# Values first, the output gate later, and longer attention waits in a two-block transformer on one core

## The chip, the core and the metric

The kernel runs on one core of a Trainium2 chip. A core has engines that work side by side, each with its own queue of instructions, taken in order: PE (TensorE) multiplies matrices and transposes, DVE (VectorE), ACT (ScalarE) and POOL (GpSimd) work on vectors, SP issues DMAs. An instruction that needs another engine's result waits for a semaphore, and everything behind it in its own queue waits with it. The metric is the device time of one launch in microseconds (us), the median of several runs.

## The reference

Two blocks of two layers each work on `x` of 256 rows and 1024 columns, all in float32. Cut to what matters here:

```
def first_block(x, ...):
    for l in range(2):
        z = rms_norm(x, attn_norm_g[l]) @ w_in[l]
        qa, ka, va, qb, kb, vb, ga, gb = split(z, [512, 128, 128, 512, 512, 512, 1024, 1024])
        qa, ka = rope(rms_norm(qa, q_norm_a)), rope(rms_norm(ka, k_norm_a))     # norm per head of 64
        ya = window_gqa(qa, ka, va, sink_a[l]) @ w_proj_a[l]                    # 8 heads, 2 of keys
        qb, kb = rms_norm(qb, q_norm_b), rms_norm(kb, k_norm_b)
        yb = neighbourhood_attn(qb, kb, vb, rel_bias_b[l]) @ w_proj_b[l]        # 8 heads
        x = x + (sigmoid(ga) * ya + sigmoid(gb) * yb) @ w_out[l]
        x = x + swiglu(rms_norm(x, ffn_norm_g[l]))

def second_block(x, ...):
    for l in range(2):
        q_a, k_a, v_a, x_m, z_m = split(x @ w_in[l], 512 each)
        y_a = dilated_attention(q_a, k_a, v_a, rel_bias)                        # 8 heads, causal
        x_c = silu(causal_conv(x_m))
        h = layer_norm(mlstm(x_c, x_m), per head) * m_norm_g
        y_m = sigmoid(z_m) * h
        g_a, g_m = split(sigmoid(x @ w_gate[l] + b_gate[l]))
        y = (g_a * (y_a @ w_br_a[l]) + g_m * (y_m @ w_br_m[l])) @ w_o[l]
        x = layer_norm(ALPHA * x + y)
        x = layer_norm(ALPHA * x + (swiglu(x) if l == 0 else moe(x)))           # moe: 8 experts, 2 of them each row
```

## The kernel before

**Matmuls.** The rows are two halves of 128, `t` = 0 and 1. Every weight comes from HBM as `raw`; ACT casts its upper part to `wh` (L218) and DVE subtracts that from it to give `wl` (L219), for 1024 columns at a time. Each product is made of three matmuls (L366 to L368: `wh` by `xTh`, `wl` by `xTh`, `wh` by `xTl`). `project` multiplies the rows by a stretch of up to 512 columns, weights block by block, and hands each finished half (in PSUM, `mm`) to a function `done(t, ps)`. With `outer=4` the last four blocks are done for half 0 first and then for half 1.

**Side work.** What is not a weight's matmul is a Python generator. `go` puts it on the list `side`, and `tick`, called after every part of `project` (two weight blocks for one half: six matmuls of 512 columns), advances each generator on it to its next `yield`. So the instructions of the side work are written among the matmuls in tick order, and engines take them in that order. `_WAIT` holds how many ticks a generator lets pass at a named place. `finish(gen)` ticks on until a generator has ended, with no matmul of weights between.

**First block.** The order of columns is q and k of the first attention (each half normalised by `head_norm`: ACT squares, DVE sums (L598), POOL takes the root (L443, L444), and after four ticks DVE multiplies (L602), which is the last reader of the PSUM buffer), then the values of the second attention (`keep_v`, columns 1792 on; the first attention's own values come with k, L844), then its q and k, then the gates. In layer 0 POOL also makes the tables of rope (L537 to L549, L540, L541), DVE the gains out of them (L586, L587) and the rotation (L609, L615, L616).

**Attention** goes in quads of four heads of one half (`softmax_quad`): scores on PE (L625), row maxima with the bias on DVE (L640), exponentials on ACT (L652), reciprocal and scaling on DVE (L656, L658), wait "s2", transposes on PE (L665), copies to SBUF by `evac`, which takes ACT (L431) and DVE (L433) in turn, wait "s3", product with the values on PE (L673), and its upper and lower parts on ACT and DVE (L677, L678). A second quad may start five ticks after the one before.

**Second block.** The order of columns is the output gate `z_m` (tanh), the convolution's input, at which the mLSTM generator `M` starts, q, k, values, at which the attention `A` starts, then four stretches of `w_gate_2`, each ended by DVE's addition of the bias (L1211) and ACT's tanh. mLSTM's output is written on DVE (L1092 to L1117). `branches` then multiplies mLSTM's output and the attention's by their weights, in this order; before the first matmul of each it calls `finish` on the generator.

Of the kernel before, what the change touches and what calls it, by code (L numbers as in the profile page):

```python
# [14 lines left out]
ALU = mybir.AluOpType  # L15
# [19 lines left out]
_WAIT = {"m15": 4, "m16": 2, "x0": 4, "t": 13, "r": 31, "g": 3, "g0": 7, "h": 3, "y": 3, "p": 2, "a0": 4, "a1": 0, "a2": 2, "q": 9, "k": 6, "b": 11, "s0": 0, "s1": 2, "s2": 4, "s3": 3, "o": 2, "mix": 3, "u": 5, "x": 3, "n0": 4, "n1": 1, "m0": 4, "m1": 1, "m2": 1, "m3": 0, "m4": 0, "m5": 2, "m6": 3, "m7": 3, "m8": 1, "m9": 4, "m10": 0, "m11": 3, "m12": 0, "m13": 7, "m14": 5}  # L35
# [233 lines left out]
class Kernel:  # L269
    def __init__(self, tc, io, upto="all", orders=None):  # L270
# [9 lines left out]
        self.ticks, self.begun, self.quads = 0, -100, 0  # L280

# [309 lines left out]
    def head_norm(self, ps, nh, scale):  # L591
# [8 lines left out]
        for _ in range(4):  # L600
            yield
# [26 lines left out]
    def softmax_quad(self, t, h0, q, k, v, bias, nk, sink, hi, lo):  # L628
# [30 lines left out]
        yield from self.wait("s2")  # L659
        PT = []  # L660
        for a in range(2):
# [4 lines left out]
            self.evac(p, pt)  # L666
            PT.append(p)
        yield from self.wait("s3")
# [11 lines left out]
    def attention(self, name, deps, q, k, v, bias, nk, sink, y, beside=None, turn=None):  # L680
# [9 lines left out]
        while jobs or live:  # L690
# [10 lines left out]
            if jobs and self.quads < (_BESIDE if beside in self.side else _QUADS) and self.ticks - self.begun > _APART:  # L701
# [5 lines left out]
                gen = self.softmax_quad(t, h0, q, k, v, bias, nk(t), sink, *out[t])  # L707
# [61 lines left out]
    def branches(self, G, which, l):  # L769

        V = self.nc.vector
        for br, (wait, y, arr, side) in enumerate(which):
# [4 lines left out]
            for n in range(2):  # L777

                def gated(t, ps):
                    z = D * side + 512 * n  # L780
# [25 lines left out]
    def first_block(self, l, xT, nxt, heads):  # L806
# [53 lines left out]
        self.project(xT, 8, W(0, 512), later(prep_q), outer=4)  # L860
        if not self.dry:
            self.stream.lead = _AHEAD
        self.project(xT, 8, W(512, 256), later(prep_k), w=256)
# [32 lines left out]
        self.project(xT, 8, W(1792, 512), keep_v)  # L896
# [249 lines left out]
    def second_block(self, l, xT):  # L1146
# [19 lines left out]
        xx, thz, convs = {}, {}, []  # L1166
# [9 lines left out]
        self.project(xT, 8, [("w_in_2", (l,), 2048, 512)], tanh_z, outer=4)  # L1176
# [3 lines left out]
        qT, kT, va = {}, {}, {}  # L1180
# [8 lines left out]
        def keep_v(t, ps):  # L1189
            va[t] = self.s2(512)  # L1190
            self.evac(va[t], ps)

        self.project_T(xT, "w_in_2", l, 0, keep(qT, 0.125))
        self.project_T(xT, "w_in_2", l, 512, keep(kT, 1.0))
        self.project(xT, 8, [("w_in_2", (l,), 1024, 512)], keep_v)
# [8 lines left out]
        ))  # L1204
        for n in range(2):
            bg = self.row(D)
            self.bcast_row(bg, io["b_gate"][l, n])
            for j in range(2):
                def gate(t, ps):
                    g = G[t][:, D * n + 512 * j : D * n + 512 * j + 512]  # L1210
                    V.tensor_tensor(g, ps, bg[:, 512 * j : 512 * j + 512], op=ALU.add)  # L1211
                    nc.scalar.activation(g, g, AF.Tanh, scale=0.5)
                self.project(xT, 8, [("w_gate_2", (l,), D * n + 512 * j, 512)], gate)
# [451 lines left out]
```

## Time and profile before

| | |
|---|---|
| median of 3 runs | 2345.89 us (2345.5 to 2346.64) |
| profiled execution | 2344.98 us, span 2343.2 us |
| mean granted clock of PE | 0.990 |
| PE busy | 2269.1 us (97%) |
| DVE busy | 1822.2 us (78%) |
| ACT busy | 1441.0 us (61%) |
| POOL busy | 100.3 us (4%) |

The span is the time from the first instruction to the last one on the core. A share is that of the span in which the engine had an instruction in work. The first block's layers, the second block's layer 0 and the token mixer of its layer 1 fill the span to about 1340 us; the experts follow.

### The profile page before, as it was taken

What the parts mean: (1) busy time and instruction counts of PE and PEld (TensorE: products, weight loads), DVE (VectorE), ACT (ScalarE), POOL (GpSimd) and SP (SyncE); (2) the same over time, 40 slices, a digit from 0 to 9 for tenths busy, and PEclk for the clock granted to TensorE, in tenths of its full rate; (3) what the DMA queues carried; (4) which work ended last, traced back from release to release, by engine and by line L of the source; (5) the groups of instructions that cost most, each with busy time, mean ns of one, the idle gap of its engine ahead of it and who ended that gap; (6) DMA issues with size and microseconds to landing.
All of it is one profiled execution on the core that took longest, in us unless ns stands there. A gap on an engine that the chain in (4) does not pass through costs nothing. (4 is left out here: it accounts for less than half of the span.)

```text
span 2343.2 us, 30976 instructions
## 1 busy us (share of the span) xinstructions
PE 2269.1 (97%) x11041; PEld 1859.9 (79%) x11041; DVE 1822.2 (78%) x2672; ACT 1441.0 (61%) x2166; POOL 100.3 (4%) x163
## 2 busy tenths in 40 slices
PE   6999999999999999999998899999999999999997
PEld 5778888778888977788886688888888888888775
DVE  5866556867565677655767799999999999999988
ACT  4555444555444554444454488888888888888775
POOL 4100001100010000000100000000000000000000
PEclk9999999999999999999999899999999999999998
DMA  6435555435565444554544799999999999999981
GB/s 238 159 138 180 182 186 204 167 126 180 180 233 205 154 136 168 197 198 164 184 168 141 300 362 371 354 370 349 371 349 370 349 373 341 376 339 376 332 334 47
DMA packets 128162, 583.06 MB, mean 249 GB/s; under 512 B 14592, under 2 KB 14880, under 8 KB 74624
## 3 DMA queue, kind: packets, MB, share of 16 engines
q1 hardware_dynamic: 124416, 566.44, 66.5%
q0 software_dynamic: 3584, 14.56, 1.9%
q8 instruction: 89, 1.46, 0.2%
q14 instruction: 73, 0.60, 0.1%
HBM read 579.90 MB, written 1.05 MB: 248 GB/s over the span
## 5 line engine op out<-in xcount | busy, mean ns | idle before, releaser
L219 DVE TENSOR_TENSOR wl<-raw,wh 128x1024 fp32r<-128x1024 f32 x594 | 711.7, 1229 | 147.8 <-ACT wh L218 145.1
L366 PE MATMUL mm<-wh,xTh 128*128 128x512 f32 (+1 forms) x1904 | 762.0, 400 | 6.7 <-DVE s L602 3.3
L367 PE MATMUL mm<-wl,xTh 128*128 128x512 f32 (+1 forms) x1904 | 742.5, 390 | 8.8 <-DVE wl L219 8.8
L218 ACT CAST wh<-raw 128x1024 fp32r<-128x1024 f32 x594 | 611.9, 1050 | 122.6 <-PE mm L368 110.0
L366 PEld LDWEIGHTS mm<-wh,xTh 128*128 128x128 f32 x1904 | 359.3, 189 | 82.6 <-issue 11.7
L367 PEld LDWEIGHTS mm<-wl,xTh 128*128 128x128 f32 x1904 | 359.8, 189 | 76.0 <-DVE wl L219 9.9
L368 PE MATMUL mm<-wh,xTl 128*128 128x512 f32 (+1 forms) x1008 | 392.4, 389 | 2.1 <-DVE xTl L455 1.9
L366 PE MATMUL mm<-wh,s 128*128 128x512 f32 x968 | 386.2, 399 | 0.0
L368 PE MATMUL mm<-wh,s 128*128 128x512 f32 x968 | 378.5, 391 | 0.2 <-DVE s L458 0.2
L367 PE MATMUL mm<-wl,s 128*128 128x512 f32 x968 | 378.0, 391 | 0.0
L368 PE MATMUL mm<-wh,xTh 128*128 128x512 f32 x896 | 349.7, 390 | 0.0
L219 DVE TENSOR_TENSOR wl<-s,wh 128x512 fp32r<-128x512 f32 x384 | 242.2, 690 | 14.1 <-ACT wh L218 10.8
L219 DVE TENSOR_TENSOR wl<-wide,wh 128x1024 fp32r<-128x1024 f32 x196 | 235.1, 1222 | 17.0 <-ACT wh L218 6.2
L218 ACT CAST wh<-s 128x512 fp32r<-128x512 f32 x384 | 217.4, 620 | 23.2 <-PE mm L368 21.7
L218 ACT CAST wh<-wide 128x1024 fp32r<-128x1024 f32 x196 | 204.1, 1055 | 36.4 <-PE mm L368 33.0
L368 PEld LDWEIGHTS mm<-wh,xTl 128*128 128x128 f32 x1008 | 190.9, 189 | 43.7 <-DVE xTl L455 4.3
L366 PEld LDWEIGHTS mm<-wh,s 128*128 128x128 f32 x968 | 182.5, 189 | 39.4 <-issue 2.5
L368 PEld LDWEIGHTS mm<-wh,s 128*128 128x128 f32 x968 | 182.1, 188 | 39.7 <-DVE s L458 0.8
L367 PEld LDWEIGHTS mm<-wl,s 128*128 128x128 f32 x968 | 182.6, 189 | 35.3
L368 PEld LDWEIGHTS mm<-wh,xTh 128*128 128x128 f32 x896 | 168.3, 188 | 36.0
L454 ACT CAST s<-ax 128x256 fp32r<-128x256 f32 x178 | 66.4, 373 | 163.5 <-PE ax L452 163.5
L455 DVE TENSOR_TENSOR s<-ax,s 128x256 fp32r<-128x256 f32 x178 | 75.1, 422 | 68.2 <-ACT s L454 68.2
(287 smaller groups left out, 1934.0 us busy)
## 6 DMA issues: line engine op xcount, KB each, us to landing
raw<-in_wpre SPq DMA_DIRECT2D x197, 1024.0 KB, 4.8
wide<-in_wexp SPq DMA_DIRECT2D x97, 1024.0 KB, 6.5
s<-in_wexp SPq DMA_DIRECT2D x384, 256.0 KB, 6.4
raw<-in_wexp SPq DMA_DIRECT2D x96, 1024.0 KB, 6.6
xTl<-in_wexp SPq DMA_DIRECT2D x24, 1024.0 KB, 6.9
bc<-in_wexp SPq DMA_DIRECT2D x44, 512.0 KB, 6.9
raw<-in_wpre SPq DMA_DIRECT2D x8, 512.0 KB, 3.5
wide<-in_bias_b POOLq DMA_DIRECT2D x2, 1536.0 KB, 9.6
```

The source lines that it names most:

```text
L218: nc.scalar.copy(h, raw)
L219: nc.vector.tensor_tensor(l, raw, h.bitcast(F32), op=ALU.subtract)
L366: nc.tensor.matmul(out, xh, wh, start=first, stop=False)
L367: nc.tensor.matmul(out, xh, wl, start=False, stop=False)
L368: nc.tensor.matmul(out, xl, wh, start=False, stop=last)
L454: nc.scalar.copy(hi, ps)
L455: nc.vector.tensor_tensor(lo, ps, hi.bitcast(F32), op=ALU.subtract)
```

## The change

- `head_norm` lets five ticks pass, not four, before DVE's multiplication.
- Waits "s2" and "s3" are 5 and 4 ticks for an attention that runs beside no other generator (the first block's two), and stay 4 and 3 (`s2x`, `s3x`) in the second block's, which runs beside mLSTM.
- Both copies of transposed probabilities are on ACT.
- First block, layer 0: the second attention's values are projected first of all, with `outer=4`; layer 1 keeps its order.
- Second block: values are projected first, the output gate after k. Attention starts ahead of the gate. The gates' tanh comes a tick after the addition. `branches` takes the attention first.

```diff
--- before.py
+++ after.py
@@ -32,7 +32,7 @@
-_WAIT = {"m15": 4, "m16": 2, "x0": 4, "t": 13, "r": 31, "g": 3, "g0": 7, "h": 3, "y": 3, "p": 2, "a0": 4, "a1": 0, "a2": 2, "q": 9, "k": 6, "b": 11, "s0": 0, "s1": 2, "s2": 4, "s3": 3, "o": 2, "mix": 3, "u": 5, "x": 3, "n0": 4, "n1": 1, "m0": 4, "m1": 1, "m2": 1, "m3": 0, "m4": 0, "m5": 2, "m6": 3, "m7": 3, "m8": 1, "m9": 4, "m10": 0, "m11": 3, "m12": 0, "m13": 7, "m14": 5}
+_WAIT = {"m15": 4, "m16": 2, "x0": 4, "t": 13, "r": 31, "g": 3, "g0": 7, "h": 3, "y": 3, "p": 2, "a0": 4, "a1": 0, "a2": 2, "q": 9, "k": 6, "b": 11, "s0": 0, "s1": 2, "s2": 5, "s3": 4, "s2x": 4, "s3x": 3, "o": 2, "mix": 3, "u": 5, "x": 3, "n0": 4, "n1": 1, "m0": 4, "m1": 1, "m2": 1, "m3": 0, "m4": 0, "m5": 2, "m6": 3, "m7": 3, "m8": 1, "m9": 4, "m10": 0, "m11": 3, "m12": 0, "m13": 7, "m14": 5}
@@ -278,6 +278,7 @@
         self.ticks, self.begun, self.quads = 0, -100, 0
+        self.late = []
@@ -597,7 +598,7 @@
         nc.scalar.activation(q, v, AF.Square, scale=scale)
         nc.vector.reduce_sum(ss, q, axis=AX.X)
         r = self.rstd(ss, (nh,), 1.0 / 64, 1e-6)
-        for _ in range(4):
+        for _ in range(5):
             yield
         nc.vector.scalar_tensor_tensor(q, v, scale, r[:, :, None].to_broadcast([128, nh, 64]), op0=ALU.mult, op1=ALU.mult)
         return q
@@ -625,7 +626,7 @@
                 self.nc.tensor.matmul(ps[a][:, i], q(t, h), k(h, nk), start=True, stop=True)
         return ps
-    def softmax_quad(self, t, h0, q, k, v, bias, nk, sink, hi, lo):
+    def softmax_quad(self, t, h0, q, k, v, bias, nk, sink, hi, lo, beside):
         nc = self.nc
         V = nc.vector
@@ -656,16 +657,16 @@
         V.reciprocal(den, den)
         for a in range(2):
             V.tensor_tensor(P[a], P[a], den[:, a, :, None].to_broadcast([128, 2, nk]), op=ALU.mult)
-        yield from self.wait("s2")
+        yield from self.wait("s2" if beside is None else "s2x")
         PT = []
         for a in range(2):
             pt = self.ax(2 * nt, 128)
             p = P[a].rearrange("p a (b c) -> p (a b) c", c=128)
             for i in range(2 * nt):
                 nc.tensor.transpose(pt[:, i], p[:, i], self.c("ident"))
-            self.evac(p, pt)
+            nc.scalar.copy(p, pt)
             PT.append(p)
-        yield from self.wait("s3")
+        yield from self.wait("s3" if beside is None else "s3x")
         po = self.ax(2, 128)
         for i in range(2):
             for kt in range(nt):
@@ -704,7 +705,7 @@
                 self.quads += 1
                 if t not in out:
                     out[t] = self.s2(4, 128, dt=F32R), self.s2(4, 128, dt=F32R)
-                gen = self.softmax_quad(t, h0, q, k, v, bias, nk(t), sink, *out[t])
+                gen = self.softmax_quad(t, h0, q, k, v, bias, nk(t), sink, *out[t], beside)
                 next(gen)
                 live.append((t, gen))
                 if not jobs and turn is not None:
@@ -777,6 +778,7 @@
             for n in range(2):
                 def gated(t, ps):
+                    self.finish(*self.late)
                     z = D * side + 512 * n
                     g = G[t][:, z : z + 512]
                     V.scalar_tensor_tensor(g, g, 1.0, ps, op0=ALU.add, op1=ALU.mult)
@@ -857,9 +859,12 @@
             V.tensor_scalar(vb[t], ps, xT.r[t], None, op0=ALU.mult)
         vb = {}
-        self.project(xT, 8, W(0, 512), later(prep_q), outer=4)
-        if not self.dry:
+        values = lambda outer: self.project(xT, 8, W(1792, 512), keep_v, outer=outer)
+        if l == 0:
+            values(4)
+        if not self.dry and l == 0:
             self.stream.lead = _AHEAD
+        self.project(xT, 8, W(0, 512), later(prep_q), outer=4 if l else 0)
         self.project(xT, 8, W(512, 256), later(prep_k), w=256)
         ya, yb, turn = {}, {}, ["a0", "a1", None]
         pa = list(prep)
@@ -893,7 +898,8 @@
                     kT2[i] = self.s2(2, S)
             return [kT2[i][:, :, 128 * t : 128 * t + 128] for i in range(2)]
-        self.project(xT, 8, W(1792, 512), keep_v)
+        if l:
+            values(0)
         self.project(xT, 8, W(768, 512), later(prep_b(put_q, gqb)))
         self.project(xT, 8, W(1280, 512), later(prep_b(put_k, gkb)))
         B = self.go(self.attention(
@@ -1163,7 +1169,7 @@
             nc.gpsimd.tensor_tensor(self.bias2, self.bias2, lc[:, None].to_broadcast([128, 8, 384]), op=ALU.add)
         bias = self.bias2
         G = [self.tl(self.keep, f"gate{t}", [128, 2 * D]) for t in range(2)]
-        xx, thz, convs = {}, {}, []
+        xx, thz, convs, gates = {}, {}, [], []
         def conv(c, ps):
             for i in range(2):
@@ -1173,11 +1179,15 @@
             thz[t] = self.s2(512)
             nc.scalar.activation(thz[t], ps, AF.Tanh, scale=0.5)
-        self.project(xT, 8, [("w_in_2", (l,), 2048, 512)], tanh_z, outer=4)
+        def keep_v(t, ps):
+            va[t] = self.s2(512)
+            self.evac(va[t], ps)
+
+        qT, kT, va = {}, {}, {}
+        self.project(xT, 8, [("w_in_2", (l,), 1024, 512)], keep_v, outer=4)
         self.project_T(xT, "w_in_2", l, 1536, conv)
         ym, ya = {}, {}
         M = self.go(self.mlstm(l, convs, xx, thz, mg, bif, wif, ym))
-        qT, kT, va = {}, {}, {}
         def keep(dst, scale):
             def f(c, ps):
@@ -1186,13 +1196,8 @@
                 dst[c // 2] = d
             return f
-        def keep_v(t, ps):
-            va[t] = self.s2(512)
-            self.evac(va[t], ps)
-
         self.project_T(xT, "w_in_2", l, 0, keep(qT, 0.125))
         self.project_T(xT, "w_in_2", l, 512, keep(kT, 1.0))
-        self.project(xT, 8, [("w_in_2", (l,), 1024, 512)], keep_v)
         half = lambda h: slice(64 * (h % 2), 64 * (h % 2) + 64)
         pair = lambda h: (h // 4, h // 2 % 2)
         A = self.go(self.attention(
@@ -1202,19 +1207,26 @@
             lambda h, kt: va[kt][:, 64 * h : 64 * h + 64],
             lambda t, h: bias[:, h, 128 * t : 128 + 256 * t], lambda t: 128 * (t + 1), None, ya, M,
         ))
+        self.project(xT, 8, [("w_in_2", (l,), 2048, 512)], tanh_z)
         for n in range(2):
             bg = self.row(D)
             self.bcast_row(bg, io["b_gate"][l, n])
             for j in range(2):
-                def gate(t, ps):
-                    g = G[t][:, D * n + 512 * j : D * n + 512 * j + 512]
-                    V.tensor_tensor(g, ps, bg[:, 512 * j : 512 * j + 512], op=ALU.add)
+                def gate(t, ps, g, b):
+                    V.tensor_tensor(g, ps, b, op=ALU.add)
+                    yield
                     nc.scalar.activation(g, g, AF.Tanh, scale=0.5)
-                self.project(xT, 8, [("w_gate_2", (l,), D * n + 512 * j, 512)], gate)
+
+                at = D * n + 512 * j
+                self.project(
+                    xT, 8, [("w_gate_2", (l,), at, 512)],
+                    lambda t, ps: gates.append(self.go(gate(t, ps, G[t][:, at : at + 512], bg[:, 512 * j : 512 * j + 512]))),
+                )
         if l % 2:
             self.load_router()
         self.mixed, self.mixed_T = {}, {}
-        self.branches(G, ((M, ym, "w_br_m_2", 1), (A, ya, "w_br_a_2", 0)), l)
+        self.late = gates
+        self.branches(G, ((A, ya, "w_br_a_2", 0), (M, ym, "w_br_m_2", 1)), l)
         g, b = self.ln_rows(l, 0)
         xT = Transposed(self, self.normed(g, b, l % 2 == 1))
         for n in range(2):
```

Where instructions stand now is shown at three places.

DVE, first block, layer 0, around q and k of the first attention (`mm` is what is read from PSUM, `wl` a weight's lower part, `tiny` a sum of squares, `rms` the row's root, `wide_74` the gains' tables). Before:

```order
L598 TENSOR_REDUCE tiny_250<-s_52_249 128x8
L602 SCALAR_TENSOR_TENSOR s_52_249<-mm_189,rms_118,tiny_253 128x512
L598 TENSOR_REDUCE tiny_283<-s_56_282 128x8
L219 TENSOR_TENSOR wl_290<-raw_91,wh_289 128x1024
L219 TENSOR_TENSOR wl_296<-raw_127,wh_295 128x1024
L219 TENSOR_TENSOR wl_300<-raw_127,wh_299 128x1024
L219 TENSOR_TENSOR wl_332<-raw_129,wh_331 128x1024
...
L565 TENSOR_SCALAR s_29_144<-s_29_144 128x64
...
L586 SCALAR_TENSOR_TENSOR wide_74<-wide_74 128x2x32
...
L602 SCALAR_TENSOR_TENSOR s_56_282<-mm_256,rms_137,tiny_286 128x512
...
L609 TENSOR_TENSOR s_77_392<-s_52_249,wide_74 128x512
```

After, the same place:

```order
L566 TENSOR_SCALAR s_29_144<-s_29_144 128x64
...
L219 TENSOR_TENSOR wl_332<-raw_129,wh_331 128x1024
L219 TENSOR_TENSOR wl_350<-raw_210,wh_349 128x1024
...
L219 TENSOR_TENSOR wl_380<-raw_210,wh_379 128x1024
L219 TENSOR_TENSOR wl_412<-raw_282,wh_411 128x1024
L846 TENSOR_SCALAR s_40_188<-mm_385,rms_118 128x128
L599 TENSOR_REDUCE tiny_429<-s_85_428 128x2
L603 SCALAR_TENSOR_TENSOR s_72_359<-mm_294,rms_118,tiny_363 128x512
L587 SCALAR_TENSOR_TENSOR wide_74<-wide_74 128x2x32
...
L846 TENSOR_SCALAR s_40_188<-mm_398,rms_137 128x128
...
L610 TENSOR_TENSOR s_91_465<-s_72_359,wide_74 128x512
...
L603 SCALAR_TENSOR_TENSOR s_75_372<-mm_301,rms_137,tiny_376 128x512
```

L598 and L602 of before are L599 and L603 now, L844 is L846, L586 is L587, L609 is L610. The multiplications of q (`s_72` and `s_75`, with `mm_294` and `mm_301`) now stand behind the splits of k's weights and behind k's first and second half, and the second one behind the gains and the rotation of the first; the tables' part on DVE (L566, L573) moved ahead of k's last split.

PE, second block, layer 0, where the gates' projections end and the first branch begins (rows of `xTh` and `xTl` are the gates', `s_` operands the branches'). Before:

```order
L366 MATMUL mm_7336<-wh_7323,xTh_6043 128x512
L367 MATMUL mm_7336<-wl_7324,xTh_6043 128x512
L368 MATMUL mm_7336<-wh_7323,xTl_6044 128x512
L452 MATMUL ax_7458<-cst_78,s_1440_7272 128x128 x4
L665 MATMUL ax_7465<-cst_78,s_1464_7400 128x128 x4
L665 MATMUL ax_7471<-cst_78,s_1465_7401 128x128 x4
L366 MATMUL mm_7455<-wh_7355,s_1446_7306 128x512
L367 MATMUL mm_7455<-wl_7356,s_1446_7306 128x512
L368 MATMUL mm_7455<-wh_7355,s_1447_7307 128x512
```

After, from the last quad's transposes on:

```order
L666 MATMUL ax_7399<-cst_78,s_1440_7279 128x128 x4
L666 MATMUL ax_7405<-cst_78,s_1441_7280 128x128 x4
L367 MATMUL mm_7382<-wh_7250,xTh_6043 128x512
...
L369 MATMUL mm_7382<-wh_7333,xTl_6044 128x512
L674 MATMUL ax_7441<-s_1440_7279,s_1244_6211 64x128
L674 MATMUL ax_7441<-s_1441_7280,s_1244_6211 64x128
...
L367 MATMUL mm_7375<-wh_7369,xTh_6043 128x512
...
L369 MATMUL mm_7382<-wh_7369,xTl_6044 128x512
L367 MATMUL mm_7478<-wh_7389,s_1333_6776 128x512
L368 MATMUL mm_7478<-wl_7390,s_1333_6776 128x512
L369 MATMUL mm_7478<-wh_7389,s_1334_6777 128x512
...
L453 MATMUL ax_7494<-cst_78,s_1450_7318 128x128 x4
```

Before, a transpose of mLSTM's output (L452) and those of a quad (L665) stood together between the last gate and the first branch, with no weight's matmul between them. Now the quad's transposes and its product with the values (L674) lie among the gates' matmuls, and mLSTM's transpose (L453) among the first branch's.

PE, first block, layer 0, the end of attention over the values of the second attention (`s_95` and `s_96` before, `s_52` and `s_54` after). Before:

```order
L665 MATMUL ax_1404<-cst_78,s_274_1309 128x128 x4
L665 MATMUL ax_1410<-cst_78,s_275_1310 128x128 x4
L366 MATMUL mm_1386<-wh_1291,s_160_761 128x512
L367 MATMUL mm_1386<-wl_1292,s_160_761 128x512
...
L368 MATMUL mm_1436<-wh_1337,s_161_762 128x512
L673 MATMUL ax_1443<-s_274_1309,s_95_478 64x128
L673 MATMUL ax_1443<-s_275_1310,s_95_478 64x128
...
L366 MATMUL mm_1429<-wh_1362,s_113_564 128x512
L367 MATMUL mm_1429<-wl_1363,s_113_564 128x512
```

After:

```order
L368 MATMUL mm_1394<-wl_1298,s_181_871 128x512
L369 MATMUL mm_1394<-wh_1297,s_182_872 128x512
L674 MATMUL ax_1445<-s_266_1287,s_52_249 64x128
L674 MATMUL ax_1445<-s_267_1288,s_52_249 64x128
...
L666 MATMUL ax_1456<-cst_78,s_287_1384 128x128 x4
L666 MATMUL ax_1462<-cst_78,s_288_1385 128x128 x4
L674 MATMUL ax_1468<-s_287_1384,s_52_249 64x128
L674 MATMUL ax_1468<-s_288_1385,s_52_249 64x128
...
L367 MATMUL mm_1444<-wh_1336,s_226_1089 128x512
L368 MATMUL mm_1444<-wl_1337,s_226_1089 128x512
```

Before, the last quad's product (L673) had matmuls of a branch on either side. Now two quads' products (`ax_1445`, `ax_1468`) and the last quad's transposes (`ax_1456`, `ax_1462`) stand behind one another between the first branch's last matmul (`mm_1394`) and the second branch's first (`mm_1444`).

## Rows read from the trace of the kernel before

**Rows 1.** Windows of the span: us, busy us (xcount) by engine, granted clock, DMA share, GB/s.

```profile
875.00:900.00 25.00, 17.92 (x98) 13.93 (x99) 17.43 (x33) 12.31 (x23) 0.54 (x1) 0.86 0.42 147
...
1390.00:1440.00 50.00, 50.00 (x226) 41.22 (x225) 46.28 (x63) 40.76 (x61) 0.00 (x0) 1.00 1.00 374
```

**Rows 2.** Waits of TensorE, 0 to 600 us: total us, times, longest.

```profile
PE mm L367 <- DVE wl L219: 8.8, 2, 8.3
...
PE mm L366 <- DVE s L602: 3.3, 2, 2.2
...
PE ax L673 <- DVE s L433: 3.0, 2, 1.5
PE ax L665 <- DVE tiny L640: 2.1, 2, 1.1
```

**Rows 3.** Timeline of PE, 38 to 44.2 us: start, duration; idle before and releaser in brackets.

```profile
39.38 0.58 PE L367 MATMUL mm<-wl,xTh 128*128 128x256 f32 x1 [8.29 <-DVE wl L219]
...
43.81 0.28 PE L366 MATMUL mm<-wh,xTh 128*128 128x256 f32 x1
```

**Rows 4.** Waits of TensorE, 600 to 1350 us.

```profile
PE ax L665 <- DVE s L658: 9.3, 2, 4.7
...
PE ax L673 <- ACT s L431: 3.5, 4, 1.5
...
PE ax L673 <- DVE s L433: 1.9, 2, 0.9
```

**Rows 5.** Timeline of PE, 880 to 895 us.

```profile
891.76 0.63 PE L367 MATMUL mm<-wl,s 128*128 128x512 f32 x1
...
893.81 0.40 PE L366 MATMUL mm<-wh,s 128*128 128x512 f32 x1
```

**Rows 6.** Timeline of POOL, 18 to 40 us.

```profile
20.80 0.37 POOL L546 TENSOR_SCALAR s<-s 128x64 f32<-128x64 f32 x1
21.26 1.22 POOL L547 TENSOR_SCALAR s<-s 128x64 f32<-128x64 f32 x1
...
35.14 1.68 POOL L444 TENSOR_TENSOR tiny<-tiny,mhalf 128x8 f32<-128x8 f32 x1
```

**Rows 7.** Timeline of DVE, 18 to 53 us.

```profile
21.15 1.22 DVE L219 TENSOR_TENSOR wl<-raw,wh 128x1024 fp32r<-128x1024 f32 x1
...
36.86 0.75 DVE L602 SCALAR_TENSOR_TENSOR s<-mm,rms,tiny 128x512 f32<-128x512 f32 x1 [12.68 <-POOL tiny L444]
...
45.63 0.23 DVE L586 SCALAR_TENSOR_TENSOR wide<-wide 128x64 f32<-128x64 f32 x1 [1.08 <-ACT wide L573]
...
47.00 0.75 DVE L602 SCALAR_TENSOR_TENSOR s<-mm,rms,tiny 128x512 f32<-128x512 f32 x1
...
48.65 0.68 DVE L609 TENSOR_TENSOR s<-s,wide 128x512 f32<-128x512 f32 x1
...
50.09 0.69 DVE L616 TENSOR_TENSOR s<-s,s 128x512 f32<-128x512 f32 x1
```

**Rows 8.** Timeline of DVE, 396 to 412 us.

```profile
409.96 0.74 DVE L602 SCALAR_TENSOR_TENSOR s<-mm,rms,tiny 128x512 f32<-128x512 f32 x1
...
411.39 0.28 DVE L598 TENSOR_REDUCE tiny<-s 128x2 f32<-128x128 f32 x1 [0.43 <-ACT s L597]
```

**Rows 9.** Timeline of ACT, 150 to 162 us.

```profile
154.17 0.49 ACT L652 ACTIVATE s<-s,tiny 128x256 f32<-128x256 f32 x1
...
156.93 1.06 ACT L218 CAST wh<-raw 128x1024 fp32r<-128x1024 f32 x1
159.78 0.59 ACT L431 COPY s<-ax 128x512 f32<-128x512 f32 x1 [1.79 <-issue]
```

**Rows 10.** Timeline of DVE, 150 to 162 us.

```profile
155.50 1.29 DVE L658 TENSOR_TENSOR s<-s,tiny 128x512 f32<-128x512 f32 x2
```

**Rows 11.** Timeline of DVE, 840 to 883 us.

```profile
863.81 1.12 DVE L1092 SCALAR_TENSOR_TENSOR wide<-ax,tiny,wide 128x129 f32<-128x129 f32 x4
...
868.31 0.17 DVE L656 RECIPROCAL tiny<-tiny 128x4 f32<-128x4 f32 x1
```

## The prediction

> **What bounds the kernel now.** I read the table of windows first. In the late window at 1390 us TensorE (PE) is busy for all 50.00 us with 226 groups of matmuls, 0.22 us each, at full granted clock; in the window at 875 us it is busy 17.92 of 25.00 us, at clock 0.86 [rows 1]. So the last part, the experts, is bound by PE without a gap, and what is saved or lost earlier reaches the end 1:1. The number of PE instructions does not change, so the change is worth the sum of the PE waits it takes away less those it makes.
>
> The views of PE's waits say where those lie. In the first 600 us, the two layers of the first block: one wait of 8.3 us for the split of a weight (L219), two for the normalisation of q (L602; 2.2 us and, the total being 3.3, 1.1 us), two of 1.5 us for the copy of the transposed probabilities by VectorE (L433), two of about 1.05 us for the row maxima (L640) [rows 2]. After that, in the second block: two waits of 4.7 us for the normalised probabilities (L658), and waits of 1.5 and 0.9 us for the copies by ScalarE and VectorE [rows 4]. All of them stand at the places that the change touches.
>
> A long wait also costs clock. After the 8.29 us wait, 20 matmuls of 256 columns start between 39.38 and 43.81, 0.22 us apart [rows 3], twice the half of 0.22 us that the 512 wide ones take at full clock [rows 1]: 2.2 us more. After the 4.7 us wait the 512 wide ones stand at 0.41 us each (five from 891.76 to 893.81) instead of 0.22 [rows 5]; six of them and eight transposes at half rate make about 2 us more. Both are the lower of the two clocks, 1.2 GHz.
>
> **The change part by part.** Each term is a saving in us, negative for a loss.
>
> *Head of layer 0.* Before, PE loses 8.3 + 2.2 + 2.2 = 12.7 us here. The cause is in VectorE's timeline: the normalisation of q stands at its queue's head for 12.68 us, waiting for POOL's reciprocal root (L444), with the next weights' splits behind it [rows 7]. POOL is late because the rope tables are ahead of that in its queue. With values first, the first 512 columns end in a scaling by the row's root alone, and the 48 matmuls of q (10.6 us at 0.22) lie beside the tables. What takes its place is seen in the new order: q's first normalisation stands behind the evacuation of k's first half, its second behind the rope gains, k's second half and the rope of q's first half. Row by row from before: gains 45.63 to 47.00, 1.37; k's scaling and sum of squares, 0.9 (from 47.75, the end of the 0.75 us normalisation, to 48.65); rope 48.65 to 50.78, 2.13; the normalisation 0.75 [rows 7]: 5.1 us. Of these the first six matmuls of the next projection (1.4 us) cover some; 3.7 are a wait. The first normalisation itself is about 0.7 late (0.9 + 0.75 after k's first half, whose second half covers 1 us). Remaining: 4.4 us. To it comes what POOL loses beside VectorE's splits: an operation of the tables took 0.37 us alone and 1.22 beside a split [rows 6], 0.85 more; four splits now stand beside the tables, 3.4 us, and the tables' end is what VectorE waits for ahead of the second half of k's weights. If all of that shows and the clock drops as well, 4.4 + 3.4 and some 2 us are left, a saving of 3; with none of it, 8.3. I take **+5** (3 to 8.3), since most of that delay has q's matmuls to hide behind.
>
> By the Trainium skill's page "SBUF — State Buffer" (Who interferes with whom), a VectorE instruction with both inputs in SBUF and a GpSimd instruction that reads SBUF shut each other out for the whole instruction. The row of 21.26 agrees: the POOL operation began 0.11 us after the split of 21.15 and ended 0.11 us after it [rows 6, 7]. By that rule, with each of six splits between 20 and 37 us costing up to a whole 1.22, the tables end 7 us later. It speaks against this edit and stands as a rival below.
>
> *Middle of both first layers.* Both copies of the transposed probabilities on ScalarE and one tick more (six matmuls, 1.4 us) before transposes and before the values' product: the waits for L433 (1.5) and L640 (1.05) go, 2.55 a layer. The second copy on ScalarE lies 0.59 us behind the first [rows 9], inside that tick. **+2.5** each, 5 in all (0 to 6; 0 if ScalarE's weight casts of 1.06 [rows 9] push the copies out by as much).
>
> *Tail of layer 0.* A quad now lives eleven ticks, not nine, and the order shows the last two quads' values products and one set of transposes between the first branch's last matmul and the second branch's first, with no weights' matmul between. Exposed: two copies (0.59 each), then the chain from the row maxima, of which four exponentials at 0.49 [rows 9] and 1.29 of normalisation [rows 10] lie partly beside PE's own 3 us of transposes and products. I count 1.2 for the copies and half of the 3.3 us chain: **-2.9** (-1.2, copies alone, to -5). Layer 1 leaves only one product there, whose cover is a tick: **0** (0 to -1.2).
>
> *Head of layer 1.* Order unchanged, but the normalisation waits five ticks. It moves behind the second half of k in VectorE's queue: it began at 409.96 and the sum that it now follows ended at 411.67 [rows 8], 1.7 us later, on top of a wait of 1.1 that is there already; with the first normalisation pushed behind the other sum too (0.7), **-2.5** (0 to -4, the latter with half clock).
>
> *Second block, each layer.* Before: 4.7 + 1.5 + 0.9 of waits [rows 4] and 2 of clock, 9.1 us. The 4.7 us wait came because three ticks of the attention had to be finished ahead of the first branch's matmuls with nothing beside them. In the new order the attention ends one tick ahead of its branch, with a wide project around every step, and mLSTM ends before its own. What stays: VectorE puts 4.5 us of mLSTM output (863.81 to 868.31) ahead of a quad's reciprocal [rows 11], so a transpose or product is still late once in a layer; I keep the 1.5 and 0.8 for it. **+6.8** a layer, 13.6 (7 to 17). Moving the output gate behind the keys and its tanh one tick later costs nothing while ScalarE has slack (12.31 us busy of 25 [rows 1]); without this cover the tanh would hold a PSUM buffer for one exponential's 0.5 us at each of four gates.
>
> Sum: 5 + 5 - 2.9 + 0 - 2.5 + 13.6 = 18.2 us. The profiled execution took 2344.98, so 2326.8; the median of the runs stands 0.9 above it, 2327.7. **Predicted 2328.**
>
> **Rivals.** *The wait comes back* in the second block: attention now runs beside the mLSTM on one VectorE queue, and the queue's lag of 4.5 us, seen once, shows in two of the four quads. For: VectorE is busy 17.43 of 25 us there [rows 1]. Against: the quads are at least five ticks apart (6.9 us), more than the lag. Then a layer gains 1.5, not 6.8: 18.2 - 10.6 = 7.6, so 2338; with the first block's gain gone too, 2343.
> *All goes*: tables hidden (+8.3), layer 1's head unharmed (0), 1 us left a layer (+8.1 each): 8.3 + 5 - 2.9 + 16.2 = 26.6, so 2319. For: the head's waits before are all of one cause. Against: the new order in VectorE's queue.
> *POOL shut out*: tables end 7 us later, the first normalisation with them, and the head of layer 0 gains 1 instead of 5, or loses 1: 14.2 to 12.2, 2332 to 2334. For: the one row that shows it. Against: POOL alone has gaps between splits to catch up in.
> *Slower*: ScalarE's two copies in series behind a weight cast (1.06 + 0.59 [rows 9]) come too late in all 24 quads. If each quad's product waits 1.2 us, 29 us are lost against 18 won: 2357. It decides from 0.76 us a quad. Against: the step before the product is now four ticks in the first block (5.5 us) and three in the second (4.1), against 0.59 + 0.59 + 1.06 = 2.2 of work.
>
> **How the numbers follow.** My forecast 0.57, the wait coming back 0.18 (0.11 of it faster by more than 0.2%, that is 4.7 us, about what a measurement of this kernel can tell from none), all goes 0.15, POOL shut out 0.05, slower 0.05. Faster: 0.57 + 0.11 + 0.15 + 0.05 = 0.88; same 0.07; slower 0.05. The range 2315 to 2338 reaches from a little beyond "all goes" to the better edge of "the wait comes back"; what it leaves out is about 0.05 below and 0.15 above.
>
> **What would show it.** Right: no wait of 8 us at the split in the first 50 us, but one of 3 to 4 us for q's second normalisation; no wait of 4.7 us for L658's successor in either second layer, and a granted clock near 1 there; a wait of 2 to 3 us between the first layer's two branches; layer 1's 1.1 us wait grown to 3. Wrong: waits of 2 us or more for ScalarE's copies in many quads; a wait of over 3 us in the second block at the mLSTM's output; a half rate stretch in the heads.

## The result and the profile after

The changed kernel took 2317.38 us (median of 4 runs, 2315.54 to 2319.82) against 2345.69 before, a ratio of 0.9881 (95% interval 0.9864 to 0.9899): 28.3 us saved. Its profiled execution spans 2314.8 us, against 2343.2.

Windows after, one on the attention's end in the second block's layer 0 and the late one, answer to [rows 1] (us, busy us by engine, granted clock, DMA share, GB/s):

```profile
858.00:883.00 25.00, 25.00 (x137) 20.66 (x136) 20.70 (x51) 14.36 (x27) 3.03 (x3) 1.00 0.47 168
1390.00:1440.00 50.00, 50.00 (x230) 41.04 (x229) 45.89 (x59) 39.70 (x56) 0.00 (x0) 1.00 0.95 345
```

PE no longer stands still where the branches begin, and the clock stays full. The views of PE's waits, the first 600 us (it answers to [rows 2]) and then from 600 to 1350 us ([rows 4]):

```profile
PE mm L367 <- DVE s L603: 8.7, 3, 3.3
PE ax L666 <- DVE s L659: 1.6, 1, 1.6
...
PE ax L626 <- ACT s L432: 0.6, 1, 0.6
PE mm L368 <- DVE wl L219: 0.5, 1, 0.5
```

```profile
PE ax L453 <- DVE x L519: 7.3, 3, 4.8
PE ax L1332 <- DVE r_sel L1329: 2.6, 1, 2.6
PE mm L369 <- DVE xTl L456: 1.1, 2, 0.6
```

In the second block no wait for a quad's probabilities or their copies is left; the three lines that head its list are of other places and stood there before. In the first block the 8.3 us wait for the split is gone, and three for q's normalisation stand in its place: 2.2 and 3.25 us in layer 0, 3.3 in layer 1.

Where the time came from is read by the start of the PE instruction of the same count in both traces (11041 in each). Saved between two counts, in us; the last column of the table is the sum that the prediction gave for the stretch:

| stretch (count) | before, from to | after, from to | saved | predicted |
|---|---|---|---|---|
| head of layer 0 (60 to 240) | 27.0 to 73.8 | 27.6 to 69.5 | 4.9 | 5 |
| rest of layer 0 (240 to 800) | 73.8 to 172.6 | 69.5 to 165.8 | 2.5 | 2.5 - 2.9 |
| head of layer 1 (1800 to 1950) | 390.2 to 419.6 | 383.4 to 416.6 | -3.9 | -2.5 |
| rest of layer 1 (1950 to 2600) | 419.6 to 536.7 | 416.6 to 529.9 | 3.9 | 2.5 |
| second block, layer 0 (3900 to 4500) | 797.9 to 911.0 | 791.1 to 894.0 | 10.1 | 6.8 |
| second block, layer 1 (5800 to 8000) | 1177.4 to 1652.4 | 1160.0 to 1624.2 | 10.8 | 6.8 |

They add up to 28.3; outside of them little moves. At count 240 the two orders differ: eight scores of the first attention (L625) stand ahead of it before, and eight wide matmuls in their place after, some 0.75 us longer (an estimate from 0.23 us a wide matmul and 0.13 a score in these traces). So of the first layer's 7.4 us the head saved nearer 5.6 and the rest 1.8.

In the second block's layer 0 PE's idle time between the two counts was 7.6 us before and is nothing after; the other 2.5 us are busy time, most of it the half clock behind the 4.7 us wait.

POOL and DVE in the head of layer 0, after (timelines; they answer to [rows 6, 7]):

```profile
29.21 0.37 POOL L541 TENSOR_SCALAR s<-s 128x64 f32<-128x64 f32 x1
29.67 1.18 POOL L542 TENSOR_TENSOR s<-s,s 128x64 f32<-128x64 f32 x1
30.93 1.10 POOL L561 TENSOR_SCALAR s<-s 128x64 f32<-128x64 f32 x1
32.12 1.23 POOL L562 TENSOR_SCALAR s<-s 128x64 f32<-128x64 f32 x1
33.42 1.09 POOL L541 TENSOR_SCALAR s<-s 128x64 f32<-128x64 f32 x1
34.60 0.32 POOL L542 TENSOR_TENSOR s<-s,s 128x64 f32<-128x64 f32 x1
...
43.22 1.69 POOL L445 TENSOR_TENSOR tiny<-tiny,mhalf 128x8 f32<-128x8 f32 x1
```

```profile
29.45 4.83 DVE L219 TENSOR_TENSOR wl<-raw,wh 128x1024 fp32r<-128x1024 f32 x4
37.54 0.20 DVE L566 TENSOR_SCALAR s<-s 128x64 f32<-128x64 f32 x1 [3.26 <-POOL s L542]
...
46.60 0.74 DVE L603 SCALAR_TENSOR_TENSOR s<-mm,rms,tiny 128x512 f32<-128x512 f32 x1
...
51.48 0.74 DVE L603 SCALAR_TENSOR_TENSOR s<-mm,rms,tiny 128x512 f32<-128x512 f32 x1
```

Four operations of the tables that ran beside the four splits from 29.45 on took 1.1 to 1.2 us, their neighbours alone 0.32 to 0.37. The tables end at 37.5 us, against 33.7 before, and DVE waited 3.26 us for them at L566. By the Trainium skill's page "SBUF — State Buffer" (Who interferes with whom), a VectorE instruction with two SBUF inputs contends with a GpSimd instruction that reads SBUF, over ports that only one of the two can hold at a time. The rows agree: the POOL operation lasts about as long as the split. They price it at about 0.8 us each, since the operation's own time falls into it.

PE behind the second normalisation of q in layer 0, and in layer 1:

```profile
52.37 0.60 PE L367 MATMUL mm<-wh,xTh 128*128 128x512 f32 x1 [3.25 <-DVE s L603]
52.78 0.63 PE L368 MATMUL mm<-wl,xTh 128*128 128x512 f32 x1
...
56.09 0.39 PE L367 MATMUL mm<-wh,xTh 128*128 128x512 f32 x1
```

```profile
406.26 0.47 PE L367 MATMUL mm<-wh,xTh 128*128 128x512 f32 x1 [3.29 <-DVE s L603]
...
408.26 0.63 PE L368 MATMUL mm<-wl,xTh 128*128 128x512 f32 x1
```

Matmuls stand 0.42 us apart (0.60 and 0.63 us each) after 52.37 until 56.09: about 1.7 us more, at the lower of the two clocks. In layer 1 the same follows five matmuls later (0.63 us at 408.26). The end of attention in layer 0:

```profile
158.19 1.23 PE L666 MATMUL ax<-cst,s 128*128 128x128 f32 x8 [1.63 <-DVE s L659]
...
160.13 1.09 PE L674 MATMUL ax<-s,s 128*64 128x128 f32 x14 [0.17 <-ACT s L667]
```

### The profile page after: what moved, and what is told of

Its sections match the earlier page's. It is cut to its first block, busy times and chain, and to the rows that moved or that the text cites. A ratio compares the mean times of both kernels' runs of the same rounds, so it can differ in the third digit from the quotient of the medians.

```text
span 2314.8 us, 30997 instructions
## 1 busy us (share of the span) xinstructions
PE 2261.4 (98%) x11041; PEld 1858.3 (80%) x11041; DVE 1808.7 (78%) x2648; ACT 1451.6 (63%) x2190; POOL 104.7 (5%) x163
## 5 line engine op out<-in xcount | busy, mean ns | idle before, releaser
L367 PE MATMUL mm<-wh,xTh 128*128 128x512 f32 x1904 | 761.1, 400 | 10.4 <-DVE s L603 8.7
L368 PE MATMUL mm<-wl,xTh 128*128 128x512 f32 x1904 | 742.1, 390 | 0.5 <-DVE wl L219 0.5
L369 PE MATMUL mm<-wh,xTh 128*128 128x512 f32 x896 | 350.1, 391 | 0.0
L219 DVE TENSOR_TENSOR wl<-s,wh 128x512 fp32r<-128x512 f32 x384 | 241.8, 686 | 14.1 <-ACT wh L218 10.7
```

What stands on the lines that cost most here:

```text
L219: nc.vector.tensor_tensor(l, raw, h.bitcast(F32), op=ALU.subtract)
L367: nc.tensor.matmul(out, xh, wh, start=first, stop=False)
L368: nc.tensor.matmul(out, xh, wl, start=False, stop=False)
L369: nc.tensor.matmul(out, xl, wh, start=False, stop=last)
```

## The experiments

Medians are of 4 runs each. The kernel before was run beside each set of four, with medians of 2346.91 (first four), 2346.19 and 2345.93 us; differences of one or two us between kernels of different sets are not told apart by the medians, so the stretches of the table above are compared as well. Those are us saved against before, in its order: head and rest of layer 0, head and rest of layer 1, second block's layers 0 and 1.

| run | median us | ratio to before (95%) | stretches |
|---|---|---|---|
| changed kernel | 2317.38 | 0.9881 (0.9864 to 0.9899) | 4.9, 2.5, -3.9, 3.9, 10.1, 10.8 |
| e1 second block alone | 2328.46 | 0.9922 (0.9905 to 0.9939) | -1.6, 0.0, 0.0, 0.0, 8.6, 9.3 |
| e2 mLSTM's branch first | 2330.52 | 0.9935 (0.9918 to 0.9951) | 5.1, 2.5, -3.9, 3.9, 3.0, 4.3 |
| e3 four ticks | 2313.66 | 0.9857 (0.9841 to 0.9874) | 5.3, 4.0, 0.0, 3.1, 10.1, 9.6 |
| e4 and rotation later | 2309.92 | 0.9842 (0.9825 to 0.9858) | 7.4, 4.0, 0.0, 3.1, 10.1, 10.2 |
| e5 branch order alone | 2356.38 | 1.0042 (1.0026 to 1.0059) | 0.0, 0.0, 0.0, 0.0, -5.8, -5.8 |
| e6 waits 4 and 3 | 2318.43 | 0.988 (0.9863 to 0.9896) | 4.9, 3.3, -4.9, 2.2, 10.1, 10.2 |
| e7 copies in turn | 2321.64 | 0.9896 (0.988 to 0.9913) | 6.5, 2.0, -3.8, 3.7, 8.6, 9.6 |
| e8 tables behind | 2306.37 | 0.9831 (0.9814 to 0.9847) | 11.5, 4.0, 0.0, 3.1, 10.1, 11.4 |
| e9 q first | 2325.43 | 0.991 (0.9893 to 0.9926) | -4.5, 3.9, -3.6, 3.9, 10.1, 10.0 |
| e10 tanh at once | 2325.47 | 0.9915 (0.9899 to 0.9932) | 5.1, 2.5, -3.8, 3.9, 5.6, 8.5 |
| e11 values first twice | 2319.6 | 0.9888 (0.9872 to 0.9905) | 4.9, 2.5, 0.7, -2.7, 10.1, 11.0 |
| e12 rotation last | 2304.95 | 0.9824 (0.9808 to 0.984) | 11.0, 4.0, 1.1, 3.1, 10.1, 10.5 |

The head of layer 0 varies by one or two us between executions of the same code: in e1 it is that of before, and cost 1.6 us more. So does the last column: it is 9.6 to 11.4 in the eight rows whose second block is the changed kernel's, while the column before it is 10.1 in all of them.

**e1, the second block's part alone** (the changed kernel with the first block, the norm's ticks, "s2", "s3" and the copies of before).

> The kernel before with the second block's part of the change alone (values first, output gate behind the keys, gates' tanh a tick later, attention's branch first); the first block, the norm's four ticks and the copies by ACT and DVE in turn stay as before. Theory (each part's waits are local and the parts add up): the second block keeps the 20.5 us that it won in the changed kernel, 10.2 a layer: about 2325 us, 20 below before. Rival (the waits for the copies, 1.5 and 0.9 us a layer, went because both copies are on ACT): they come back here, 15 to 16 us below before, with two waits of PE for copies in each layer.

18.4 us below before: between the two. A layer saved 8.6 and 9.3 us, one and a half less than in the changed kernel, with one wait of 0.6 us for DVE's copy (L434) in each. The parts do nearly add up: 17.9 here and 7.4 for the first block in the changed kernel, of 28.3.

**e2, mLSTM's branch first again.**

```diff
-        self.branches(G, ((A, ya, "w_br_a_2", 0), (M, ym, "w_br_m_2", 1)), l)
+        self.branches(G, ((M, ym, "w_br_m_2", 1), (A, ya, "w_br_a_2", 0)), l)
```

> The changed kernel with mLSTM's branch first again. Theory (the early start of the attention is what counts; it has ended by then in either order): what is left is mLSTM's own end, one transpose with its two copies of about 1.2 us, with no matmul beside: 1.5 to 2.5 us a layer lost against the changed kernel, 3 to 5 in all. Rival (the order of the branches is what took the 4.7 us wait and its 2 us of clock away): 6.5 us a layer lost, 13 in all.

13 us slower than the changed kernel, 6.5 to 7 a layer: the rival's number. PE there in layer 0:

```profile
876.00 0.63 PE L453 MATMUL ax<-cst,s 128*128 128x128 f32 x4 [0.71 <-DVE s L1123]
...
880.66 0.80 PE L367 MATMUL mm<-wh,s 128*128 128x512 f32 x1 [2.66 <-ACT s L458]
```

The attention's last product ended near 872.3; PE waits for mLSTM's own end instead, 0.7 us for its transpose's operand and 2.7 for the copy of what was transposed, and half clock follows. So the wait at the first branch does not belong to the attention: whichever is finished last must not be multiplied first. How long it lasts is not mLSTM's doing alone. ACT there:

```profile
877.96 1.23 ACT L1218 ACTIVATE gate<-gate 128x512 f32<-128x512 f32 x2 [4.24 <-DVE gate L1216]
...
880.02 0.59 ACT L458 ACTIVATE s<-ax 128x512 fp32r<-128x512 f32 x1
```

The transpose was done at 876.6, and its copy (L458) stood until 880.02 behind two tanh of the gates, which waited for DVE, and a cast of 1.03 us. The theory's 1.5 to 2.5 us a layer counted the copies without this queue; no run took the tanh out of their way, so the order's price without it is open.

**e5, the order of the branches alone**, in the kernel before (the reverse edit of e2).

> The kernel before with nothing but the attention's branch first in the second block. Theory (early start and order of the branches work together: first there is the branch whose operand is ready): here the attention still has a quad's transposes and product to do when its branch begins, so the 4.7 us wait stays, a second one of 1.3 us for the copies follows: 2 to 6 us slower than before. Rival (the order of the branches alone takes the wait away): 10 us or more faster than before.

10 us slower than before, the theory's direction at about twice its size. PE's waits from 600 us on:

```profile
PE ax L665 <- DVE s L658: 8.4, 2, 4.7
...
PE ax L673 <- ACT s L431: 7.3, 6, 2.1
PE ax L673 <- DVE s L433: 3.5, 4, 0.9
```

The long wait stays (3.8 us in layer 0, 4.7 in layer 1), and to the copies' come two more of 1.7 and 2.1 us by ACT and two of 0.8 by DVE. The order pays only with the early start; the early start alone (e2) kept 3.0 and 4.3 us a layer.

**e10, the gates' tanh at once.**

```diff
                     V.tensor_tensor(g, ps, b, op=ALU.add)
-                    yield
                     nc.scalar.activation(g, g, AF.Tanh, scale=0.5)
```

(cut; `gate` is then called at once and is not put on the list of side work).

> The changed kernel with the gates' tanh in the same tick as the addition. Theory (ACT has slack there): within 1 us of the changed kernel. Rival (the tanh then stands ahead of the weights' casts or the copies and waits for DVE at the head of ACT's queue, beside mLSTM): waits of PE for ACT's copies or for the casts in the second block, 1 us a layer or more, 2 to 5 us slower.

8 us slower by the medians, 6.6 by the stretches: more than the rival gave. ACT in layer 0, and PE beside it:

```profile
866.02 0.63 ACT L1217 ACTIVATE gate<-gate 128x512 f32<-128x512 f32 x1 [5.83 <-DVE gate L1216]
866.55 0.49 ACT L653 ACTIVATE s<-s,tiny 128x256 f32<-128x256 f32 x1
```

```profile
869.70 1.23 PE L666 MATMUL ax<-cst,s 128*128 128x128 f32 x8 [2.41 <-DVE s L659]
...
871.16 0.63 PE L368 MATMUL mm<-wl,xTh 128*128 128x512 f32 x1
```

The tanh stands at the head of ACT's queue for 5.83 us, waiting for DVE's addition, which has mLSTM's output ahead of it. The quad's exponentials behind it could have run: with the tanh a tick later they do, at 860.38, and the tanh waits behind them:

```profile
860.38 0.51 ACT L653 ACTIVATE s<-s,tiny 128x256 f32<-128x256 f32 x1
...
866.29 0.63 ACT L1218 ACTIVATE gate<-gate 128x512 f32<-128x512 f32 x1 [3.36 <-DVE gate L1216]
```

In the kernel before, ACT's timeline shows the same just ahead of the 4.7 us wait of [rows 4]:

```profile
885.92 0.63 ACT L1212 ACTIVATE gate<-gate 128x512 f32<-128x512 f32 x1 [5.92 <-DVE gate L1211]
886.45 0.49 ACT L652 ACTIVATE s<-s,tiny 128x256 f32<-128x256 f32 x1
```

What this costs is read on DVE, at the quad's reciprocal, which needs the exponentials: before, with the tanh at once (e10), and in the changed kernel:

```profile
888.54 0.18 DVE L656 RECIPROCAL tiny<-tiny 128x4 f32<-128x4 f32 x1 [2.66 <-ACT s L652]
```

```profile
868.65 0.18 DVE L657 RECIPROCAL tiny<-tiny 128x4 f32<-128x4 f32 x1 [2.67 <-ACT s L653]
```

```profile
866.18 0.17 DVE L657 RECIPROCAL tiny<-tiny 128x4 f32<-128x4 f32 x1
```

So of the 4.7 us before, the tanh's place accounts for about 2.7; the other 2.0 are DVE's own queue, which had mLSTM's output, a split and the gate's addition between the row maxima and the reciprocal. That division is an estimate: the tanh alone was not moved in the kernel before.

**e3, four ticks in the norm** (`range(5)` in `head_norm` back to `range(4)`).

> The changed kernel with the head norm's four ticks of before. Theory (the fifth tick puts the multiplication behind the second half of k on DVE): layer 1's wait of 3.3 us and the half rate behind it go back to the 1.1 us of before, 3.9 us won; in layer 0 the first wait (2.2 us) falls to under 1, the second (3.25 us) stays, as the rotation is still ahead of it: 4 to 6 us faster than the changed kernel. Rival (the fifth tick hides POOL's root in the heads of the second attention, where DVE would wait for it at the head of its queue): 2 us or more are given back there and the sum is within 2 us of the changed kernel.

3.7 us faster than the changed kernel. The head of layer 1 is back at 0.0, 3.9 us won, as the theory had it; in layer 0 the first wait falls to 0.5 us and the second grows to 4.4, so the head wins nothing. The rest of layer 0 wins 1.5: the first scores stand one tick (six matmuls) earlier, and the tail's 1.6 us wait is gone. The rest of layer 1 gives 0.8 back, where a wait of 0.7 us for ACT's copy (L667) has come up.

**e4, the rotation a tick later too.**

```diff
-            yield
+            for _ in range(2):
+                yield
             self.rope(qn, 8, gains["q"], t, qn)
```

with "q" 8 ticks, not 9.

> As the one before, and the rotation of q a tick later (its wait after it a tick shorter), so that the second normalisation of q stands ahead of the first half's rotation on DVE. Theory: in layer 0 the second wait of 3.25 us with its half rate stretch of 1.8 us falls to about 1 as well: 8 to 10 us faster than the changed kernel, 2307 to 2309. Rival (the heads wait for POOL's root, not for DVE's order): the second wait stays at 2 us or more, and the time within 2 us of the run with four ticks alone.

7.5 us faster than the changed kernel. Both waits in layer 0, on PE's timeline:

```profile
46.73 0.47 PE L367 MATMUL mm<-wh,xTh 128*128 128x512 f32 x1 [0.53 <-DVE s L603]
...
50.69 0.47 PE L367 MATMUL mm<-wh,xTh 128*128 128x512 f32 x1 [2.33 <-DVE s L603]
```

The second is 2.3 us, not 1, and half clock still follows it: between theory and rival. DVE's order was part of it. The rest is e8's question.

**e8, DVE's part of the tables behind** ("t" 22 ticks, not 13, on top of e4).

> The run with four ticks and the rotation later, and DVE's part of the rope tables nine ticks later, behind both normalisations of q. Theory (DVE's wait of 3.3 us for POOL's tables holds back q's sums and so POOL's roots): the waits of 0.5 and 2.3 us for q's normalisation fall under 0.5 each: 2 to 3 us faster than that run, about 2307. Rival (POOL is the limit: its tables end at 38 us and each root takes 1.9): DVE then waits for the root at the head of its queue, the waits come back at the weights' split, and the time is within 1 us of that run or above it.

3.5 us faster than e4, 11 faster than the changed kernel. DVE in the head of layer 0:

```profile
43.01 0.74 DVE L603 SCALAR_TENSOR_TENSOR s<-mm,rms,tiny 128x512 f32<-128x512 f32 x1
...
45.78 0.74 DVE L603 SCALAR_TENSOR_TENSOR s<-mm,rms,tiny 128x512 f32<-128x512 f32 x1
...
47.42 0.18 DVE L566 TENSOR_SCALAR s<-s 128x64 f32<-128x64 f32 x1
```

Both normalisations come before the tables' part (L566) and end at 43.8 and 46.5 us; neither wait is left. POOL's roots were late because DVE's queue, waiting for POOL's tables, held back the sums that they are made from. The first sum on DVE, in e4 and here:

```profile
43.06 1.27 DVE L599 TENSOR_REDUCE tiny<-s 128x8 f32<-128x512 f32 x2
```

```profile
39.57 0.69 DVE L599 TENSOR_REDUCE tiny<-s 128x8 f32<-128x512 f32 x1 [2.29 <-ACT s L598]
```

The tables themselves end later here, at 39.6 us against 38.4, since six splits now run beside them. So their end was not the limit, and the rival is out.

**e12, the rotation three ticks later still** (5 ticks, "q" 5).

> The fastest run so far (tables behind, four ticks, rotation later) with the rotation of q three ticks later still, so that in layer 1 too q's second normalisation stands ahead of the rotation of the first half. Theory: layer 1's wait of 1.1 us goes, 1 us faster than that run. Rival (the rotation then delays the first attention's start): 1 us or more slower.

1.4 us below e8, which the medians of different sets do not tell from none. Layer 1's wait is gone and its head 1.1 better, and a wait for the rotation (L617) of 1.1 us shows in layer 0, whose two stretches stay within 0.5 of e8's:

```profile
PE ax L465 <- DVE s L617: 1.1, 1, 1.1
...
PE ax L666 <- ACT s L667: 0.7, 1, 0.7
```

This is the lowest median: 0.9824 of before, 12 us under the changed kernel.

**e9, q first in layer 0.**

> The changed kernel with q first in layer 0 as before. Theory (values first is what hides POOL's tables): the 8.3 us wait for the weights' split and its 2 us of clock come back, and the second wait for q's normalisation, which has the rotation and k's second half ahead of it with five ticks, is 4 to 5 us: the head of layer 0 loses 15 us instead of 7.6, 7 to 9 us slower than the changed kernel. Rival (what the splits beside the tables cost POOL has eaten most of the gain): within 3 us of the changed kernel.

8 us slower, as the theory had it. The head of layer 0 loses 4.5 us against before instead of saving 4.9, or 5.6 at the same place in the order. The rest saves 3.9 for the changed kernel's 1.8, without the tail's 1.6 us wait:

```profile
PE mm L367 <- DVE s L603: 7.9, 2, 4.6
PE mm L368 <- DVE wl L219: 7.7, 1, 7.7
```

**e11, values first in layer 1 too.**

> The changed kernel with values first in layer 1 of the first block too. Theory (in layer 1 no tables delay POOL, and q then ends right ahead of k as in layer 0): the wait for q's first normalisation, 0 now, becomes 0.5 to 1, the second stays at 3.3, so no gain: 0 to 3 us slower. Rival (values give POOL and DVE 11 us more room at the start of a layer as in layer 0): 2 us or more faster.

2.2 us slower, as the theory had it: layer 1's head and rest together lose 2.0 against before, where they were even in the changed kernel (the order at their border differs, so only the sum compares). The waits for q's normalisations are 0.5 and 3.3 us.

**e6, "s2" and "s3" at 4 and 3**, and **e7, copies by ACT and DVE in turn** (`self.evac(p, pt)`).

> The changed kernel with the two waits of the first block's attention at 4 and 3 ticks again. Theory (the tick more is what covers the copies and the row maxima in the first block): waits of 1 us for transposes and products come back, 2 to 2.5 us a layer, the wait of 1.8 us at the end of layer 0 goes to about 1: 3 to 5 us slower than the changed kernel. Rival (both copies on ACT are what counts): within 1.5 us of the changed kernel.

> The changed kernel with the copies by ACT and DVE in turn again. Theory (in the first block the tick more covers a copy by either engine, in the second block DVE lags beside mLSTM): first block the same within 1 us, second block 1.3 us a layer lost as in the run with the second block's part alone: 2 to 3 us slower than the changed kernel. Rival (DVE's copy is late everywhere): 1.5 us a layer lost in the first block too, 5 to 6 us in all.

e6 is within 1.1 us of the changed kernel, as its rival said: with both copies on ACT, the tick more is worth 1.7 us in the rest of layer 1 and costs 0.8 in that of layer 0, where the tail is longer. e7's median is 4 us up, between theory and rival, but its stretches add up to 1.8 us less than the changed kernel's; the rests of the first block's layers lose 0.5 and 0.2, and the second block has DVE's two waits in view:

```profile
PE ax L674 <- DVE s L434: 1.2, 2, 0.6
```

So in the first block either remedy does most of it, and in the second the copies on ACT are worth 1.5 us in layer 0, and as much in layer 1 as far as its column can tell.

## Why the prediction was right

The direction, the range and five of the six stretches' signs held; the size was 28.3 where 18.2 was summed. The time is that of "all goes" by a different account, since layer 1's head was harmed after all, and it lies only 2.4 us inside the range's better end: that the range held with one term so far off is in part luck. One sign that was given for being wrong did show, the half rate stretches in the heads.

*Head of layer 0: as worked out, the figure with some luck.* 4.9 for 5, which was picked between 3 and 8.3. Values first does hide the tables (e9), four splits cost POOL four times some 0.8 us, and the new waits stand where the order had put them. Their sizes were 2.2 for 0.7 and 3.25 for 3.7, with half clock. Most of the first is the fifth tick's (0.5 with four, e3). What the prediction missed is how the tables reach PE: not by their end itself, but by DVE's waiting for it ahead of the sums (e8).

*Head of layer 1: mechanism right, size off*: -3.9 for -2.5, since the 3.3 us wait was followed by half clock, the far end of the bound. e3 shows that the fifth tick is all of it.

*Middle and tail of the first block: the sum was too low.* 2.5 (1.8 without the shift at count 240) for -0.4, and 3.9 for 2.5. The tail waits 1.6 and 0.2 us, not 2.9; with four ticks in the norm (e3), or waits of 4 and 3 (e6), the 1.6 is gone. In the rest of layer 1 PE's idle time fell by 2.4 us, from 3.0 to 0.6, as summed; the other 1.5 are busy time over as many instructions of each kind, for which the prediction had no term and whose cause no run isolates.

*Second block: the step that failed* is "Moving the output gate behind the keys and its tanh one tick later costs nothing". The gates' tanh a tick later does not cost; it wins. With the tanh at once (e10) the second block saves 5.6 + 8.5 = 14.1 us, about the 13.6 that was forecast, and keeps a wait of 2.4 us a layer, about the 2.3 that was kept; with the tick it saves 20.9 and has no wait (25.00 of 25 us busy). The prediction put the 4.7 us wait down to three ticks with nothing beside them. That was about half: ACT's queue was held 5.92 us by the tanh ahead of the quad's exponentials, and DVE's lag beside mLSTM reached PE by that way too. So the forecast fits e10 better than the kernel that it was made for, and e10's 2.4 us are the tanh's doing, not only mLSTM's output ahead of the reciprocal. The lag itself is still there: the tanh still waits 3.4 us, with nothing urgent behind it.

*"POOL shut out"* was half right in its cause and not in its price: POOL was slowed as it said, but by five splits between 20 and 37 us, not six, and one of the five was there before; the head saved 4.9, not 1. In e8 six splits stand beside the tables and PE waits for neither normalisation, so there the slowing cost PE nothing. *"The wait comes back"* and *"slower"* are shown wrong by the lists of waits, which have none of theirs; e5 shows that the change in the order of the branches alone would have been slower.

Still open: whether POOL's slowing costs PE anything in the changed kernel, where no run took it away by itself; where the busy time of the first block went; and what the tanh a tick later would give in the kernel before.

## What to carry to other kernels

In an engine's in-order queue, look at what stands behind an instruction that waits for a lagging engine: put the work whose result is wanted soon ahead of it, even if it is made a tick later. Multiply first what is ready first, and check both operands' ends, since here reordering the consumers (e5) helped only with the producers moved too. A wait read as "nothing beside it" on PE should be followed back through the releaser's releaser before it is priced.

## What the runs showed of the hardware that was not expected

The same wait cost different clocks. In e10, PE waited 2.41 us in the second block's layer 0 and 2.40 in its layer 1, for the same instruction. Windows around the two:

```profile
866.00:876.00 10.00, 7.59 (x30) 5.81 (x29) 5.18 (x8) 7.51 (x16) 0.83 (x2) 0.83 0.27 67
1240.00:1254.00 14.00, 11.60 (x66) 9.05 (x65) 9.34 (x16) 8.63 (x18) 2.21 (x6) 1.00 0.47 164
```

The first was followed by eight 512 wide matmuls 0.43 us apart (granted clock 0.83 in the stretch), the second by none (1.00): 2 us of difference. After waits of 3.25 us and more in the two heads of the first block half rate followed in every run here; for shorter ones it did in some (2.33 us in e4) and not in others (2.18 us before, 1.98 in e7), so a price for the clock is a range.
